# Five requests of sixteen 512-byte writes queued between the first loads of an RMS-norm kernel

## The chip, the cores and the metric

The kernel runs on one core of a Trainium2 chip. The metric is device time in microseconds (us), as median over runs; the profile is one run of the same program, and its span leaves out about 1.8 us of the measured time.

## The reference

```python
x: (16, 1024, 512) float32; gamma: (512,) ones; eps: 1e-5
rms = np.sqrt(np.mean(x ** 2, axis=-1, keepdims=True) + eps)
x_norm = x / rms * gamma
return np.maximum(x_norm, 0).astype(np.float32)
```

33.5 MB come in and 33.5 MB go out; each element is used once.

## The kernel before

The 16,384 rows are cut into eight chunks of 4 MB: 128 partitions with 16 rows (32 KB) each. Six chunk-sized slots lie in on-chip memory and every chunk is worked on in place. All loads and stores are issued by SyncE ("SP"), on one queue. Chunk 0 is loaded in two halves.

```python
loads = [(0, 0, G), (0, G, K - G)] + [(i, 0, K) for i in range(1, nchunks)]   # G = 8, K = 16
...
for m, (i, a, r) in enumerate(loads):
    if i < nslots:                      # nslots = 6
        load(m)
nxt = nslots
for i in range(nchunks):
    nc.sync.wait_ge(done, per * (i + 1))
    store(i)
    if i >= 1 and nxt < nchunks:
        nc.sync.wait_ge(sem_st[nxt - nslots], 16)
        for m, (c, a, r) in enumerate(loads):
            if c == nxt:
                load(m)
        nxt += 1
```

ScalarE squares and sums each row and takes the root, VectorE takes the reciprocal, scales by gamma and clips at zero. Below, "load k" is the load of chunk k (for chunk 0 its second half), "store k" the store of chunk k.

## Time and profile before

| | before |
|---|---|
| median of the first 3 runs | 162.89 us |
| span of the profiled run | 161.2 us |
| VectorE, ScalarE busy | 126.0 us (78%), 86.3 us (54%) |
| time of the main queue's packets, as a share of 16 engines' span | 97.4% |
| mean rate over the span | 416 GB/s |

An engine that is busy for 78% and ends 15 us early does not set the time of a kernel whose queue is busy for 97.4% and ends last.

### The profile page before, as it was taken

To read this page: it belongs to the slowest core of one execution; us is meant where nothing else is said; L and a number is where in the kernel's file an instruction comes from. 1 tells how busy PE (TensorE), PEld (TensorE's weight loads), DVE (VectorE), ACT (ScalarE), POOL (GpSimd) and SP (SyncE) were. 2 spreads that over 40 slices of the span, in tenths; PEclk is the share of its full clock that TensorE was granted. 3 is DMA by queue.
4 is the path that set the end of the run, shared out by engine and by line. 5 is a ranking of instruction groups with operands and counts; after the bars stand their busy time and mean duration, and the time that the engine had idled before them with its cause. 6 is when DMAs were issued, how large, how long until landed. Compare 5 with 4: busy or idle time off the path is not lost. (4 is left out here: it accounts for less than half of the span.)

```text
span 161.2 us, 1006 instructions
## 1 busy us (share of the span) xinstructions
DVE 126.0 (78%) x164; ACT 86.3 (54%) x273; POOL 0.2 (0%) x4
## 2 busy tenths in 40 slices
DVE  1103989898989898999999999999999999993000
ACT  3088929889988988988900298503994000000000
POOL 0000000000000000000000000000000000000000
DMA  5999999999999999999999999999999999999993
GB/s 155 433 439 431 496 390 415 496 390 399 512 390 390 512 399 390 390 399 512 390 399 504 399 399 496 407 399 488 407 407 488 407 407 480 415 407 464 431 390 138
DMA packets 2456, 67.12 MB, mean 416 GB/s; under 512 B 276, under 2 KB 276, under 8 KB 280
## 3 DMA queue, kind: packets, MB, share of 16 engines
q1 hardware_dynamic: 2448, 67.11, 97.4%
q10 hardware_dynamic: 8, 0.01, 0.0%
HBM read 33.56 MB, written 33.55 MB: 416 GB/s over the span
## 5 line engine op out<-in xcount | busy, mean ns | idle before, releaser
L115 ACT ACTIVATE junk<-slots 128x512 f32 x128 | 74.5, 582 | 30.8 <-ACTq L111 30.5
L139 DVE SCALAR_TENSOR_TENSOR slots<-slots,rstd,gamma_sb 128x512 f32 x128 | 86.2, 747 | 4.8 <-DVEq L136 4.8
L146 DVE TENSOR_SCALAR slots<-slots x16 | 36.7, 2294 | 2.4 <-DVEq L145 0.2
L115 ACT ACTIVATION_READ_ACCUMULATOR junk<-slots x128 | 23.9, 187 | 0.0
L133 DVE RECIPROCAL rstd<-rms x16 | 3.2, 197 | 6.4 <-DVEq L129 6.4
L122 ACT ACTIVATE rms<-ss,eps_sb x16 | 4.8, 301 | 3.0 <-ACTq L121 3.0
L126 DVE LOAD_MASK_SELECT gamma_sb<-gseed x1 | 0.0, 14 | 5.8 <-DMA gseed<-in_gamma_dram 5.8
L107 ACT ACT_TABLE_LOAD x1 | 1.3, 1283 | 2.8 <-issue 2.8
L100 DVE MEMSET gseed<- 128x512 f32 x1 | 0.5, 485 | 1.1 <-SPq L81 1.1
L126 DVE STREAM_SHUFFLE gamma_sb<-gseed 128x512 f32<-128x512 f32 x1 | 0.7, 716 | 0.0
L168 POOL MEMSET const-bfloat16-1.0<- 128x1 bf16 x1 | 0.1, 102 | 0.0
L168 POOL MEMSET const-uint8-127<- 128x1 uint8 x1 | 0.1, 102 | 0.0
L168 POOL MEMSET const-float32-1.0<- 128x1 f32 x1 | 0.1, 99 | 0.0
L168 POOL MEMSET const-float32-0.0<- 128x1 f32 x1 | 0.1, 98 | 0.2 <-issue 0.2
L101 DVE MEMSET eps_sb<- 128x1 f32 x1 | 0.1, 59 | 0.0
## 6 DMA issues: line engine op xcount, KB each, us to landing
out_dram<-slots SPq DMA_DIRECT2D x8, 4096.0 KB, 31.4
slots<-in_x_dram SPq DMA_DIRECT2D x7, 4096.0 KB, 30.4
slots<-in_x_dram SPq DMA_DIRECT2D x2, 2048.0 KB, 9.7
gseed<-in_gamma_dram ACTq DMA_DIRECT2D x1, 8.0 KB
```

The lines of the kernel that those rows point to most:

```text
L100: nc.vector.memset(gseed, 0.0).then_inc(sem_z, 1)
L101: nc.vector.memset(eps_sb, eps).then_inc(sem_e, 1)
L107: nc.scalar.preload_act_table(ACTF.Sqrt)
L115: a = nc.scalar.activation(out=junk[:, j, :], in_=slots[:, bass.ds(base + j * d, d)], func=ACTF.Square, accum_out=ss[:, bass.ds(col + j, 1)])
L122: nc.scalar.activation(out=rms[:, bass.ds(col, G)], in_=ss[:, bass.ds(col, G)], func=ACTF.Sqrt, bias=eps_sb, scale=inv_d).then_inc(sq, 1)
L126: nc.vector.stream_shuffle(gamma_sb, gseed, [0] * 32)
L133: nc.vector.reciprocal(out=rstd[:, bass.ds(col, G)], in_=rms[:, bass.ds(col, G)]).then_inc(sv, 1)
L139: r = nc.vector.scalar_tensor_tensor(out=row, in0=row, scalar=rstd[:, bass.ds(col + j, 1)], in1=gamma_sb, op0=ALU.mult, op1=ALU.mult)
L146: nc.vector.tensor_scalar_max(out=blk, in0=blk, scalar1=0.0).then_inc(done, 1)
L168: nc = _bacc.Bacc("TRN2", target_bir_lowering=False, num_devices=1)
```

## The change

Intent, as far as the code tells: the output is first written some 60 us into the run, and whatever that first write costs is to be paid earlier, by a few tiny writes among the first loads. They write zeros to the start of some rows of chunk 0; the real store overwrites them. So that two writes to the same bytes cannot race, store 0 now waits for the small ones.

```diff
+    zeros = singles.tile([16, 128], F32, name="zeros")
...
+    sem_w = tc.alloc_semaphore("touch")
+    sem_wz = tc.alloc_semaphore("touchz")
...
+        ntouch = 0
         for m, (i, a, r) in enumerate(loads):
             if i < nslots:
                 load(m)
+                if i < nslots - 1 and a + r == K:
+                    if ntouch == 0:
+                        nc.sync.wait_ge(sem_wz, 1)
+                    nc.sync.dma_start(out=ov[0][0:P:P // 16, ntouch, 0:128],
+                                      in_=zeros).then_inc(sem_w, 16)
+                    ntouch += 1
+        nc.sync.wait_ge(sem_w, 16 * ntouch)
...
+        nc.vector.memset(zeros, 0.0).then_inc(sem_wz, 1)
         nc.vector.memset(gseed, 0.0).then_inc(sem_z, 1)
```

The condition holds for loads 0 to 4, so there are five requests of sixteen rows of 512 bytes.

## The prediction

> **What bounds the kernel now.** I read the page first (its slices, the queue table, the table of costly groups and the table of issues), then the chain that ended last, then the waits of the issuing sequencer, its timeline, and windows around the first store; after that the records of single DMA packets and of semaphore increments, which those views are made from.
>
> The slices say which resource never rests:
>
> ```profile
> span 161.2 us, 1006 instructions
> DVE  1103989898989898999999999999999999993000
> ACT  3088929889988988988900298503994000000000
> DMA  5999999999999999999999999999999999999993
> DMA packets 2456, 67.12 MB, mean 416 GB/s; under 512 B 276, under 2 KB 276, under 8 KB 280
> q1 hardware_dynamic: 2448, 67.11, 97.4%
> ```
>
> The DMA row is at 9 from the second slice to the last but one: 33.5 MB in and 33.5 MB out on one queue, 97.4% of the time of 16 engines. VectorE stops some 15 us before the end, ScalarE earlier. The packet records agree: the first data packet starts at 1.95 us, the last store lands at 160.04 us, and the packets of 32 KiB (1920 of them, median 1213 ns) follow each other without a hole. Eight such packets per engine make one chunk of 4 MB, 8 x 1.213 = 9.70 us, and the landings of the loads of chunks 0 to 4 are 9.71 to 9.72 us apart. Sixteen chunk transfers (eight loads, eight stores) at 9.70 are 155.3 us, from 1.95 us on: 157.2; the records end 2.8 us later. Some of that is start-up, and 0.5 us is one stall, which matters here (below).
>
> The chain that ended last is of no help, and that is itself to be noticed: it follows engines, and the last of them is done at 146.49 us, with the last store still behind another in the queue.
>
> ```profile
> 2 pieces in order of time: start us, us, what
> 144.12 0.08 issue
> 144.20 2.29 DVE slots L146
> ```
>
> So the bound is the single queue. The sequencer's timeline shows how far ahead of the engines it is filled:
>
> ```profile
> start us, us, engine line op out<-in xcount [idle before <-releaser]
> 0.94 3.59 SPq L74 DMA_DIRECT2D slots<-in_x_dram  x7
> 31.14 16.83 SPq L78 DMA_DIRECT2D out_dram<-slots  x2
> 72.07 0.34 SPq L74 DMA_DIRECT2D slots<-in_x_dram  x1
> ```
>
> All seven first loads (24 MB, six chunks) are issued by 4.5 us and keep the engines busy until 62.32 us, when the last of them lands. Store 0 is issued at 31.14 us and store 1 at 47.62 us, but they stand behind those loads: store 0 lands at 72.06 us, one chunk after load 5. So store 0 was queued 31 us before it could begin.
>
> **The one irregularity that the change can aim at.** Load 5, the last before the first store, lands 10.21 us after load 4 (52.11 to 62.32), not 9.71: half a microsecond more than its sisters. The windows show the dip:
>
> ```profile
> 52.00:58.00 6.00, 5.55 (x8) 5.31 (x17) 0.00 (x0) 1.00 1.01 437
> 58.00:60.00 2.00, 2.00 (x4) 1.94 (x7) 0.00 (x0) 1.00 1.07 377
> 60.00:62.00 2.00, 1.85 (x4) 2.00 (x8) 0.00 (x0) 1.00 1.07 393
> ```
>
> From 437 GB/s to 377 and 393, with a DMA share that stays at 1: the packets are not absent, they are longer. Between 58 and 61 us, 26 packets of load 5 take over 1230 ns and up to 1956, the last or the last two on each engine ahead of the first store packet. No later change from loads to stores does that: at 89 to 91 us (load 6 to store 2) the excess is 30 to 160 ns on six packets, and load 6 and store 2 together land 19.51 us after store 1, against 2 x 9.70 = 19.41. So there is a once-only cost of the first store of about 0.5 us. I take it that the small early writes are meant to pay it beforehand.
>
> **What the Trainium skill says.** "DMA: Bandwidth & Descriptors", section "Queues, rings and completion order": on each DMA engine descriptors are consumed in ring order, and the semaphore increment lands only after every earlier write from that engine. The trace agrees on the order: store 0, issued at 31.14, lands only after load 5. Hence a small write placed after load i cannot land before load i has been through. The same page, section "Why a DMA increments its semaphore by 16 and not by 1": the engine count is the largest number up to 16 that divides the slowest dimensions. A 16-row write therefore puts one 512-byte row on each of 16 engines; no run shows it yet. The same page, "Specifications": 512 B is the least size without a read-modify-write, so these rows are just at the good side. And its section "Anatomy of one DMA — SWDGE (gpsimd) path" puts most of a fixed 2 us down to the write receipt, worst for HBM. That is latency, and the trace shows it does not stop the queue: load 6, right behind store 1, lands 9.54 us after it.
>
> **The change part by part.**
> Removed: nothing. All 67.1 MB still move, in the same order.
>
> Added on VectorE: one memset of 16 x 128 ahead of the two others. The 128x512 memset takes 485 ns and the 128x1 one 59 ns; this lies between, about 0.1 to 0.15 us as an estimate. It delays the gamma load by that, which lands at 7.37 us, while the first VectorE work on data starts at 14.97. Free.
>
> Added on the sequencer: the last load of each of chunks 0 to 4 is followed by one small write (the condition holds for five of the seven loads, so five writes of sixteen rows, 80 rows, 41 KB in all), a wait for the zeros ahead of the first, and a wait for all five ahead of store 0. An issue costs 0.33 to 0.72 us in this trace, mostly 0.43. Five are 2.2 us, so load 5 is issued at about 6.5 us, not 4.1. It is needed at 52. The zeros are ready at about 1.3 us, before the second load's issue ends at 1.81. Free.
>
> Moved: store 0 now waits until write 4, which stands behind load 4, has landed. Load 4 lands at 52.1; with 1 us for the write, store 0 is issued at about 53 instead of 31, and store 1 at 53.5 instead of 47.6. Load 5 occupies the engines until 62.3, so 9 us are left. Free.
>
> Added on the bound, the DMA engines: five times, per engine, one packet of 512 B and one semaphore packet (9 ns in the records of 4 B). The nearest sized record is gamma's, 2048 B in 84 ns; by size a 512 B one would be 21 ns, and with a fixed part perhaps 60. The turns from load to write and back, at the 0.10 us found above for load 6 and store 2 together, are added: 5 x (0.03 to 0.07 + 0.05 to 0.1) = 0.4 to 0.85 us, of which a half overlaps, I guess: **+0.2 to +0.5 us**.
>
> The once-only 0.5 us: if the first small write pays it, it moves from 60 us to about 13 us. But the queue is as saturated at 13 us as at 60, so a stall of the engines costs the same there: **0**. If it is only latency for a small write, which the next loads run past, the gain is up to **0.5 us**. If the stall belongs to a full-sized store and is not removed, 0. I put -0.15 on it.
>
> Sum: 162.89 + 0.35 - 0.15 = about **163.1 us**.
>
> **The rivals.**
> (1) *The warm-up works.* The small writes absorb the first-store stall out of the path; the time becomes 162.4 to 162.6. For it: the stall is seen just once, before the first store. Against it: the same serial queue carries the small writes. Even so it is 0.3%, never 2%.
> (2) *Each small write stalls its engine* like the first store, because each turns the engine from reading HBM to writing it: 4 more stalls of 0.5 us, 162.89 + 2.0 = 164.9; with a full write round trip of 1 us each it would be 167 to 168. Against it: the later turns cost 0.1 us, and load 6 behind store 1 loses nothing.
> (3) *The new wait takes over*: store 0 late enough to let the queue run dry. It would need the last write to land after 62 us, so 10 us later than load 4. Nothing in the trace suggests that; it would show as a hole of DMA.
> (4) *VectorE becomes the bound.* A stall at 13 us also delays compute. The last VectorE operation ends at 146.49 and the last store is issued at 146.52, but the store ahead of it lands at 150.37, so 3.8 us are to spare; a slip of 0.5 us is hidden.
>
> **Range and chances.** The centre is 163.1. Downwards there are 0.5 us of stall to win: low 162.4. Upwards I allow that turns cost double what I took and that the stall is not removed, +1.1: high 164.0. A change of 2% is 3.3 us. Faster by that would need more than there is of irregular DMA time; slower would need rival 2 in its worst form. Chances: faster 0.01, same 0.97, slower 0.02.
>
> **What would show it.** Right: five writes on the sequencer's timeline by 7 us, store 0 issued at 52 to 54, DMA rows still 9 throughout, 80 packets of 512 B, landings of loads 1 to 4 apart by 9.75 to 9.85 where a small write lies between, and the 26 long packets around 60 us gone or moved to around 13 us. Wrong: a hole in the DMA row after 52 us (the new wait), landings of loads apart by 10.2 or more (every write stalls), VectorE ending after 150 us, or long packets unchanged at 60 us (then the stall is of the full-sized store, and the small writes are only a cost).

## The result

The changed kernel takes 162.88 us (median of 6 runs, 162.79 to 163.12), the kernel before 162.99 us in the same rounds (162.83 to 163.12). The ratio is 0.9996, 95% interval 0.9983 to 1.0008: the same. (Ratios here are the mean time of one kernel's fast runs over that of the other's of the same rounds, so they are not quite the ratio of the medians quoted.) The interval is worth -0.28 to +0.13 us.

The page of the changed kernel, first the lines that answer to those of before, then a line of the group table and one of the issue table:

```profile
span 161.0 us, 1013 instructions
...
DVE  1103989898989899999999999999999999993000
ACT  2088929889988988988900198503994000000000
...
DMA  5999999999999999999999999999999999999993
...
DMA packets 2616, 67.16 MB, mean 417 GB/s; under 512 B 356, under 2 KB 436, under 8 KB 440
...
q1 hardware_dynamic: 2608, 67.15, 97.5%
...
L113 DVE MEMSET zeros<- 16x128 f32 x1 | 0.2, 165 | 1.0 <-SPq L84 1.0
...
out_dram<-zeros SPq DMA_DIRECT2D x5, 8.0 KB, 29.0
```

160 packets more on the queue (2608 against 2448): 80 of 512 B and 80 of 4 B, the semaphore increments. The busy rows are those of before, but for single slices of VectorE and ScalarE that differ by a tenth. The memset took 165 ns. The "29.0" in the last line is issue to landing of a small write: nearly all of it is standing behind loads.

The timeline of the issuing sequencer (start, duration, line, operation):

```profile
0.94 0.86 SPq L77 DMA_DIRECT2D slots<-in_x_dram  x2
1.85 0.42 SPq L94 DMA_DIRECT2D out_dram<-zeros  x1
...
5.75 0.44 SPq L94 DMA_DIRECT2D out_dram<-zeros  x1
6.24 0.45 SPq L77 DMA_DIRECT2D slots<-in_x_dram  x1
52.31 0.82 SPq L81 DMA_DIRECT2D out_dram<-slots  x2
71.99 0.34 SPq L77 DMA_DIRECT2D slots<-in_x_dram  x1
```

Loads and small writes alternate; the last load is issued at 6.24 us (4.08 before). Stores 0 and 1 are issued at 52.31 and 52.70 in place of 31.14 and 47.62. The sequencer's own waits name the cause:

```profile
SPq L81 <- DMA out_dram<-zeros: 21.2, 1, 21.2
```

A wait of 21.2 us is new on the sequencer, and the next line of the timeline shows that it cost nothing: store 0 landed, and with it load 6 was issued, at 71.99 us, against 72.07 before.

The windows around the first store (columns: window, its length, busy time of VectorE, ScalarE and GpSimd, clock, DMA share, GB/s; a packet's bytes are booked where it starts):

```profile
52.00:58.00 6.00, 5.55 (x8) 5.31 (x17) 0.00 (x0) 1.00 1.01 437
58.00:60.00 2.00, 2.00 (x4) 1.95 (x7) 0.00 (x0) 1.00 1.06 393
60.00:62.00 2.00, 1.85 (x4) 2.00 (x7) 0.00 (x0) 1.00 1.02 393
```

The dip ahead of store 0 is still there. The packet records say the same: 16 packets of load 5 that start at 59.8 to 60.2 us take 1361 to 2060 ns in place of 1213 (26 packets, up to 1956 ns, in the kernel before). The landings, as means over the 16 engines' semaphore increments in the trace (here and below of the one profiled run of each kernel), taken as differences from load to load:

```
            load 0>1  1>2   2>3   3>4   4>5 (last before store 0)
before        9.71   9.71  9.71  9.72   10.26
changed       9.71   9.73  9.73  9.74   10.11
```

A small write between two loads costs 0.02 us, the first one nothing that can be seen, and the stall of about half a microsecond, the long packets ahead of store 0, did not move to the first small write.

### The profile page after: what moved, and what is told of

Same layout as the page of the kernel before. It is cut to its first block, busy times and chain, and to the rows that moved or that the text cites. A ratio compares the mean times of both kernels' runs of the same rounds, so it can differ in the third digit from the quotient of the medians.

```text
span 161.0 us, 1013 instructions
## 1 busy us (share of the span) xinstructions
DVE 126.2 (78%) x165; ACT 86.3 (54%) x273; POOL 0.2 (0%) x4
## 3 DMA queue, kind: packets, MB, share of 16 engines
q1 hardware_dynamic: 2608, 67.15, 97.5%
```

## The experiments

Ten kernels, all with correct results. Where a difference of times is given, it is between medians of the same rounds, unless it is called a difference of ratios. The kernel before lay between 162.74 and 162.96 us in these rounds.

### What one small write costs: eight and four in a row

touch40: eight small writes after each of loads 0 to 4, to separate places of chunk 0.

```diff
-                    nc.sync.dma_start(out=ov[0][0:P:P // 16, ntouch, 0:128], ...
-                    ntouch += 1
+                    for q in range(8):
+                        c0 = (ntouch // K) * 128
+                        nc.sync.dma_start(out=ov[0][0:P:P // 16, ntouch % K, c0:c0 + 128], ...
+                        ntouch += 1
```

> Eight small writes in place of one after each of the first five loads: forty in all. In the changed kernel a small write is a 27 ns packet and a 9 ns semaphore packet on each engine and nothing more. Theory A (a small write costs its packets, some 36 ns of queue, and no turn): loads 0 to 4 land about 9.70 + 8 x 0.036 = 9.99 us apart, the time is 35 x 0.036 = 1.3 us over the changed kernel, about 164.1. Theory B (the cost of a write is hidden because it is a single one and fits between two loads; eight in a row expose a turn to writing of 0.1 us or a receipt of about 1 us): apart by 10.5 or more, time 166 or more. Theory C (engines absorb them altogether): 163.0. In all of them I expect the long packets ahead of store 0 to stay.

Measured: 166.00 us against 162.74 (ratio 1.0195, interval 1.0180 to 1.0211). Loads 0 to 5 landed 10.33 to 10.35 us apart in the mean of the engines, so eight writes cost 0.63 us or 80 ns each; on the engine that lands last it was 10.55 to 10.57, or about 105 ns each. Theory A (36 ns) fell, C too. B's time came (166 or more), and its distance of 10.5 on the last engine, though not in the mean; its two reasons are not told apart by this run. All records of the 512-byte packets are 27 ns, also here; what grew are the load packets behind each group (up to 1.74 us). The engines also drifted apart: the increments of one load spread over 0.46 us at load 0 and 2.5 us at load 5, and the spread stays to the end (2.8 us at the last store, 1.3 us in the kernel before), where the slowest engine sets the time. My expectation that the long packets ahead of store 0 would stay was wrong too. The windows, in the first of which the packets behind the first group are long, and in the second of which load 5 ends and store 0 begins:

```profile
13.00:16.00 3.00, 1.14 (x3) 2.52 (x10) 0.00 (x0) 1.00 0.95 361
...
60.00:66.00 6.00, 5.55 (x8) 5.53 (x20) 0.00 (x0) 1.00 1.01 437
```

A dip now stands behind each group of writes (the packet records show five bunches of long packets, one per group) and none at the turn to the stores.

touch20: the same with `range(4)`.

> Four small writes after each of the first five loads, twenty in all. One per load moved the landings apart by about 0.025 us, eight per load by 0.64 us in the mean of the 16 engines and 1.0 us over load 1's last landing to load 2's (10.56 against 9.71 for the slowest engine). The completions of eight writes in a row came 0.18 us after each other. Theory A (every write costs its 80 ns, the single one is a lucky exception): apart by 10.02 in the mean, time about 1.6 us over the kernel before. Theory B (writes in a row are worked off one per 0.18 us, and the loads behind them can start without waiting for the first 0.8 us or so of that): four are 0.72 us and nearly hidden, apart by 9.8 to 9.9, time 0.2 to 0.7 us over.

Measured: 163.22 us against 162.77 (ratio 1.0030, 1.0017 to 1.0043). Loads landed 9.81 to 9.83 us apart: 0.11 us for four writes, or 27 ns each, which is the length of their packets. Theory B holds in its numbers. So the cost is about its packet, 27 ns or less, up to four in a row, and 80 to 105 ns each at eight in a row; the bend lies between. B's reason, that completions are worked off one per 0.18 us and the loads behind have some slack for that, fits (behind load 0 the completions of four are 0.18 to 0.22 us apart, those of eight 0.17 to 0.27), but only these two counts were tried. That it goes by requests and not by packets fits too: early_64k, below, puts eight such packets on each engine in one request, and that costs 0.15 us. With four in a row the stall ahead of store 0 was there (load 5 landed 10.10 us after load 4).

### The two halves of the wait

touch_far: the small writes go to the last chunk, and the wait stands ahead of the last store.

```diff
-  out=ov[0][0:P:P // 16, ntouch, 0:128]
+  out=ov[nchunks - 1][0:P:P // 16, ntouch, 0:128]
...
-        nc.sync.wait_ge(sem_w, 16 * ntouch)
...
             nc.sync.wait_ge(done, per * (i + 1))
+            if i == nchunks - 1:
+                nc.sync.wait_ge(sem_w, 16 * ntouch)
             store(i)
```

> The five small writes go to rows of the last chunk in place of the first, and the wait for them stands ahead of the last store instead of the first. This takes the new wait alone away. If the wait ahead of store 0 is free, as the prediction says, store 0 is issued at 31 us again and the time is that of the changed kernel, 162.7 to 162.9. The long packets of load 5 at about 60 us should stay: also if the place of the small writes mattered, since they now touch other rows. If the wait had cost something, the time falls by it.

Measured: 162.97 us against 162.77 (ratio 1.0015, 1.0002 to 1.0028), store 0 issued at 31.02 us. Taking the wait away won nothing. Load 5 landed 10.30 us after load 4, so the stall stays with small writes elsewhere.

wait_only: the kernel before with the wait and no small writes.

```diff
+        nc.sync.wait_ge(sem_ld[nslots - 1], 16)    # load 4
         nxt = nslots
```

> The kernel before with a wait for load 4 ahead of store 0 and no small writes: the new wait alone. Store 0 issued at 52.2 us in place of 31.1. If the wait is free: 162.7 to 162.9, long packets on load 5 at about 60 us as before. If the early issue of store 0 mattered (prepared behind the loads), the first store starts late and the time rises by up to 1 us.

Measured: 162.88 us against 162.77 (ratio 1.0013, 0.9997 to 1.0028). The sequencer's timeline:

```profile
52.06 0.82 SPq L78 DMA_DIRECT2D out_dram<-slots  x2
72.04 0.34 SPq L74 DMA_DIRECT2D slots<-in_x_dram  x1
```

Store 0 is issued 21 us later than in the kernel before and lands at the same time (72.04 against 72.07). The wait is free. The stall is at its old place (10.21 us from load 4 to load 5).

### The wait one load later

touch_last: a sixth small write, behind load 5, so that the wait can end only when the loads are through.

```diff
-                if i < nslots - 1 and a + r == K:
+                if i < nslots and a + r == K:
```

> One more small write, behind load 5 too (six in all), so that the wait ahead of store 0 can end only after load 5. This makes rival 3 of the prediction real. Theory A (the wait then empties the queue): store 0 is issued at about 62.3, its first packet starts about 1 us later as after the very first issue (0.94 to 1.95 us), a hole of about 1.2 us in all stands in the DMA records at 62 to 63 us, and the time rises by 0.7 us (if the hole takes the place of the half microsecond of long packets) to 1.2 us (if it adds to it): 163.6 to 164.1. Theory B (the queue hides it): store 0 issued at 62 without a hole, 162.9. Load 5 should show no long packets if these come from the store packets behind it, and keep them if they are of load 5 itself.

Measured: 165.51 us against 162.74 (ratio 1.0170, 1.0156 to 1.0184): +2.8 us where I expected 0.7 to 1.2. The sequencer's timeline, then windows of the same run:

```profile
61.99 0.82 SPq L81 DMA_DIRECT2D out_dram<-slots  x2
```

```profile
61.00:62.00 1.00, 0.85 (x2) 1.00 (x4) 0.00 (x0) 1.00 0.04 8
62.00:63.00 1.00, 1.00 (x1) 0.95 (x4) 0.00 (x0) 1.00 1.23 524
79.00:84.00 5.00, 4.70 (x7) 1.61 (x6) 0.00 (x0) 1.00 0.91 315
89.00:94.00 5.00, 4.94 (x8) 0.00 (x0) 0.00 (x0) 1.00 1.04 367
```

The queue ran dry: the last packets of load 5 end at 61.3 us at the latest, the write behind them lands at 61.97, store 0 is issued at 61.99, and its first packets start at 62.83. On the average engine that is a hole of 1.74 us, not the 1.2 I had put down: I had counted the issue, and not the time from the last packet to the landing. Load 5 has no long packet (9.72 us after load 4). That is the half microsecond I had hoped for, but it came back with more: at 81 to 83 us, where load 6 first follows a store, and at 90 to 92, where store 2 follows that load, there are long packets (up to 2345 ns) where the kernel before has only two over 1300 ns, up to 1371. The same windows of the kernel before:

```profile
79.00:84.00 5.00, 4.70 (x7) 1.74 (x7) 0.00 (x0) 1.00 0.97 419
89.00:94.00 5.00, 4.79 (x8) 2.15 (x7) 0.00 (x0) 1.00 0.98 419
```

Store 1 landed 10.52 us after store 0 (9.98 before) and load 6 another 10.68 (9.43 before), 1.8 us of the loss. Hole and long packets make 3.5 us; less the stall of 0.5 us that is gone from load 5, that is the 3.0 us by which the mean landing of the last store came later (162.06 against 159.06).

gap_only: the wait for load 5 alone, no small writes.

```diff
+        nc.sync.wait_ge(sem_ld[nslots], 16)        # load 5
         nxt = nslots
```

> The kernel before with a wait for load 5 ahead of store 0 and no small writes: the empty queue of touch_last alone. touch_last took 165.5 us: a hole of 1.7 us at 62 us, no long packets on load 5, and long packets at 81 to 83 and 90 to 92 us in their place. If the hole and what follows come from the wait alone, this gives 165.2 to 165.6 with long packets at the same later places. If the small writes have a part in it, the time is 0.5 us or more below, and the long packets elsewhere.

Measured: 165.32 us against 162.96 (ratio 1.0137, 1.0114 to 1.0159), with a hole of 1.64 us and long packets at 81 to 83 and 90 to 92 us. In windows:

```profile
61.00:62.00 1.00, 0.85 (x2) 1.00 (x5) 0.00 (x0) 1.00 0.01 0
...
79.00:84.00 5.00, 4.70 (x7) 1.65 (x6) 0.00 (x0) 1.00 0.92 328
89.00:94.00 5.00, 4.87 (x8) 0.00 (x0) 0.00 (x0) 1.00 0.99 328
```

So the wait alone, by the queue that it empties, makes 2.4 of touch_last's 2.8 us. The intervals of the two ratios (1.0156 to 1.0184 and 1.0114 to 1.0159) just overlap, so a part of the small writes in the other 0.4 us is neither shown nor excluded.

### What the stall belongs to

slots5: the kernel before with five slots, so that the first store follows load 4 at 52 us. The next three kernels are slots5 with one early write between load 2 and load 3, to rows of the last chunk; of their edits only the write and the wait for it are shown, and the tile of zeros, its memset and the semaphores are left out.

```diff
-    nslots = 6
+    nslots = 5
```

> The kernel before with five slots in place of six and no small writes: the first store then follows load 4 at about 52 us, not load 5 at about 62. If the long packets belong to the first turn from loads to a full-sized store, they appear at 49 to 52 us, on load 4, and load 4 lands 10.2 us after load 3. If they belong to load 5, its place in memory or the time of about 60 us, they stay at 58 to 61 us or vanish. Time 162.9 to 163.2 in both, as the queue stays full.

early_store: a write of 4 MB.

```diff
                 load(m)
+                if i == 2:
+                    nc.sync.wait_ge(sem_wz, 1)
+                    nc.sync.dma_start(out=ov[nchunks - 1], in_=zeros).then_inc(sem_w, 16)
+        nc.sync.wait_ge(sem_w, 16)
```

> As slots5, with one full-sized store (4 MB of zeros, to the rows of the last chunk, overwritten by the real store at the end) queued between load 2 and load 3. It costs about 9.7 us of the queue, so about 172.7. Theory A (once only: the first full-sized store pays the half microsecond): long packets on load 2 at about 30 to 32 us, none on load 4 ahead of store 0. Theory B (every first turn from a row of loads to stores pays): long packets at both places, one half microsecond more. Theory C (it belongs to the output rows of chunk 0): long packets only ahead of store 0.

early_512k: `out=ov[nchunks - 1][:, 0:2, :]`, 512 KB.

> As early_store (five slots), with the early store cut from 4 MB to 512 KB (4 KB per partition, eight packets of 4 KB on each engine). It costs about 1.2 to 1.3 us of queue. The full early store made load 2 land 10.53 us after load 1 and left load 4 at 9.72. If the half microsecond is paid by the first write whatever its size, as long as it is more than a few hundred bytes per engine: load 2 late by 0.5 to 0.8 us, load 4 at 9.72, time 1.2 us over slots5. If it takes a run of full-sized stores: load 2 on time and load 4 at 10.3, the same time; or part on each side.

early_64k: `out=ov[nchunks - 1][:, 0:1, 0:128]`, 64 KB in eight packets of 512 B on each engine.

> As early_512k, with the early write cut to 64 KB: 512 bytes per partition, eight packets of 512 B on each engine in one request, the packet size of the small writes of the change. Queue cost by the packets about 8 x 27 ns = 0.22 us. Early_512k made load 2 land 10.34 us after load 1 and left load 4 at 9.73. If any run of writes pays the once-only stall, load 2 is late by 0.4 to 0.6 us and load 4 at 9.72. If it takes a certain amount of data, the eight packets pass like the small writes (load 2 at 9.7, load 3 later by about 0.2) and load 4 is at 10.3. The time is about 163.4 in both, 0.2 over slots5.

Measured, with the landings again as means over the engines:

| | time (ratio to before) | load 1 to load 2 | load 3 to load 4 (ahead of store 0) |
|---|---|---|---|
| slots5 | 163.19 (1.0027) | 9.71 | **10.32** |
| early_store, 4 MB | 173.34 (1.0658) | **10.53** | 9.72 |
| early_512k | 164.41 (1.0101) | **10.34** | 9.73 |
| early_64k | 163.41 (1.0022) | 9.73 | **10.33** |

The windows show the dip at one of the two places, never at both: at 28 to 33 us, where load 2 ends, and at 48 to 53 us, where load 4 ends. First slots5, then early_512k, then early_64k:

```profile
28.00:33.00 5.00, 4.55 (x6) 4.53 (x16) 0.00 (x0) 1.00 0.97 419
48.00:53.00 5.00, 5.00 (x8) 4.53 (x16) 0.00 (x0) 1.00 0.89 315
```

```profile
28.00:33.00 5.00, 4.55 (x6) 4.53 (x16) 0.00 (x0) 1.00 0.96 351
48.00:53.00 5.00, 5.00 (x8) 4.53 (x16) 0.00 (x0) 1.00 0.97 419
```

```profile
28.00:33.00 5.00, 4.55 (x6) 4.52 (x16) 0.00 (x0) 1.00 1.02 433
48.00:53.00 5.00, 5.00 (x8) 4.53 (x16) 0.00 (x0) 1.00 0.90 321
```

With five slots the stall moved with the first store, from load 5 at 60 us to load 4 at 50: it is neither load 5's own nor tied to the time of 60 us. With an early write of 4 MB or 512 KB it moved to that write, and the first real store had none, so with a full queue it is paid once and not at every turn from a row of loads to a store; and as the early write went to other rows, it is not bound to chunk 0's. An early write of 64 KB did not take it. It passed like the small writes of the change: loads 2 and 3 were 9.85 us apart, 0.14 more than 9.71.

And moving the stall wins nothing. early_512k costs 1.2 us over slots5 by the difference of ratios (0.0074 of 162.8), which is what its bytes need: its landing is 1.27 us after load 2's. early_store costs 10.3 us by the same sum, for 9.7 us of packets. The ratios of early_64k (0.9997 to 1.0048) and slots5 (1.0011 to 1.0042) can't be told apart.

What was not settled: why a first large write slows the load ahead of it; where between 64 KB and 512 KB the bend lies; and why it is absent in touch40, where eight requests after one load wrote just as many bytes as early_64k's one, but the engines had also drifted apart. It may be the sum of what was written that counts: touch40 had written 328 KB before store 0, more than touch20's 164 KB, which left the stall in place, and less than the 512 KB that took it; no run separates this from the drift. Open is also why it comes later and larger when the store begins on an empty queue.

## Why the prediction was right

**The bound.** The serial, full queue was the right reading. Everything that is not queue time was free as worked out: VectorE's memset (165 ns, a little over the estimate), the later issues (load 5 at 6.24 us, "about 6.5"), and the new wait (store 0 at 52.31, "about 53"). That the wait is free is not only read from a trace: wait_only and touch_far take it alone and away, and neither gains or loses more than 0.3%. Rival 3 becomes real as soon as the wait moves past load 5: touch_last and gap_only cost 2.4 to 2.8 us. The reason the change is free there is the 9 us of load 5 still in the queue.

**The cost of a small write** was over-estimated. The step was "5 x (0.03 to 0.07 + 0.05 to 0.1)" with half of it hidden. The packet is 27 ns, and the second term, the turn from reading to writing and back, is not there for writes of this size: one costs 0.02 us or less, and four in a row 27 ns each. Five come to at most 0.1 us in place of 0.2 to 0.5. Had the turn been real, touch20, with five turns and twenty packets, would have cost 5 x 0.1 + 20 x 0.027 = 1.0 us; it cost 0.45. The 0.1 us was itself a misreading: 19.51 us from store 1 to store 2 is what the last engine shows, on which the drift of the engines counts too; in the mean of the engines the same trace has 19.42, against 19.41 without a turn. Rival 2 (a stall at each write) is thereby out for this change, though eight in a row do cost more than their packets.

**The stall.** The prediction left it open between three cases, with -0.15 us on their mixture. The case that held is the one it put at 0: the stall belongs to a store of some size and the small writes do not pay it. The changed kernel's load 5 came 10.11 us after load 4, against 10.26, but touch_far, with the same small writes, had 10.30, and wait_only, with none, 10.21; so the 0.14 us is not shown to be more than scatter. (Of the runs in which the last load before store 0 is late, the two with small writes to chunk 0 itself, the changed kernel and touch20, have the lowest values, 10.11 and 10.10; the others have 10.21 to 10.33. With one trace each, a small part paid by writes to the same chunk is not excluded.) The test written down beforehand for this ("long packets unchanged at 60 us, then the stall is of the full-sized store, and the small writes are only a cost") is what came, and it stood under "Wrong". Of the signs listed under "Right", loads 9.75 to 9.85 us apart did not come either (9.73 to 9.74). So the bound and the free parts were right as mechanisms; the two small terms were not. Rival 1 fails for two reasons, each sufficient: 512 B per engine and even 4 KB per engine in one request are too little to pay the stall (early_64k), and a write that is large enough pays it on the same full queue (early_512k).

**The sum.** 162.89 + 0.35 - 0.15 = 163.1 was the forecast. The measured terms are +0.1 and 0, so about 163.0; the result is 162.88 beside 162.99 for the kernel before, with an interval that just contains +0.1. Both terms were too large in size and of opposite sign, and that they partly cancelled is luck; but neither could have come near the 3.3 us of a 2% change.

No version tried beats the two. The stall is the one irregularity the change could aim at, 0.5 us or 0.3%, and what removed it from its place cost as much or more. A larger unevenness, which the change does not touch, stands at the end of the kernel before: its last store lands 0.98 us later on the slowest engine than in the mean of the 16; for load 5 it was 0.2 us.

## What to carry to other kernels

When one queue is full from start to end, ask of each change only how many microseconds of that queue it adds or takes; moving a stall along the queue moves nothing in the time. A wait on the issuing sequencer was free here while a load with more than 9 us to go still stood in the queue, and cost the drained hole and what follows it (1.7 us, and 2.4 to 2.8 in all) as soon as nothing did. Before trying to warm something up, find out by one experiment how large a first access must be to pay the cost: here one write of 64 KB was too small and one of 512 KB did it, and five times 8 KB left the stall where it was.

## What the Trainium skill lacked or had wrong

- "DMA: Bandwidth & Descriptors", section "Queues, rings and completion order", has nothing on a once-only slow-down of the loads ahead of the first large write of a run: 0.4 to 0.8 us here in full-queue runs, taken by a first write of 512 KB or 4 MB and not by one of 64 KB.
- The same page, section "Anatomy of one DMA — SWDGE (gpsimd) path", gives about 2 us as the fixed cost of a DMA. In a full queue a small write (8 KB, HWDGE) costs at most 0.03 us, singly or four in a row; its landing comes 0.18 us after the load's ahead of it. Eight in a row cost 80 to 105 ns each. The page does call the fixed cost completion latency; it doesn't say how much of it is left in a full queue, or that small requests cost more from some number in a row.
- No page that I looked up says what follows when the queue runs dry between a load and a store. The hole itself, 1.64 and 1.74 us from the last packet to the next, is of the size of the fixed cost above; the other 1.8 us, of long packets at the next turns in touch_last, are in no page.
